# Rotary logits of latent attention: from three products over 64 partitions to two over 128

## The chip, the core and the metric

The kernel runs on one core of a Trainium2 chip. The metric is the device time of one execution in microseconds (us), the median of several runs. The engines are named as in the profile: PE (TensorE's products), PEld (its weight loads), DVE (VectorE), ACT (ScalarE), POOL (GpSimd), SP (SyncE, which issues most DMAs). ACT issues some DMAs, too; such an issue is shown as ACTq.

## What is computed

The program is a model of two blocks. First block: a short convolution mixer, a feed-forward network, latent attention (MLA) over shared keys and values, a second feed-forward network. Second block: a mixer with three branches (spatial gating, stick-breaking attention, dilated attention) and a third feed-forward network. 512 tokens, width 1024, float32. The change is in the latent attention, whose logits have two parts, one of 128 dimensions with keys of each head's own and a rotary one of 64 dimensions with one key for all eight heads:

```python
q = (rms_norm(x_n @ w_dq, q_norm) @ w_uq).reshape(bsz, seq, N_HEADS, QK_NOPE_DIM + QK_ROPE_DIM)
q_nope = q[..., :QK_NOPE_DIM]
q_rope = apply_rope(q[..., QK_NOPE_DIM:], cos[:, None, :], sin[:, None, :])
...
    s = (jnp.einsum('bqhd,bkhd->bhqk', qn, k_nope)
         + jnp.einsum('bqhr,bkr->bhqk', qr, k_rope)).astype(jnp.float32) * scale
    s = jnp.where(k_pos[None, :] <= q_pos[:, None], s, -jnp.inf)
    p = jax.nn.softmax(s, axis=-1).astype(v.dtype)
    return jnp.einsum('bhqk,bkhd->bqhd', p, v)
```

## The kernel before

Every product keeps float32's accuracy by a split: a tile x is cast on ACT to the rounded type fp32r (the high part, xh), DVE subtracts that from x (the low part, xl), and three products are summed in PSUM: high by high, low by high, high by low (`mm3`, lines 155 to 159; `split_to`, lines 119 to 133; the stationary operand is named second in the profile, as in `sc<-kh,qh`). Weights come by DMA from SP as slabs of up to 1 MB into one of two buffers (`raw`, line 139) and are split in the same way (lines 147 and 149, `whi` and `wlo`).

`layer_b` (line 532) holds the attention. It first makes the latent vectors `cq` and `ckv` and the rotary key, `kr` (lines 558 to 560). The key's 64 rows stand twice on the 128 partitions, since its weight columns were doubled. Then it goes over four pairs of heads. `project(pr)` (line 568) makes a pair's operands: a product group for the rotary part of both heads (64 rows each, together 128 partitions, copied to `x` at line 577), two groups for q, two for k, four for v. `rope` (line 522) swaps halves of 32 rows by four small DMAs of 64 KB, issued from ACT (`swap`, lines 518 and 519), and does three operations on DVE (lines 527 to 529); line 596 splits the result into `qr`, tiles `rh` and `rl`. `attend` (line 618) is called once per head: for each of four blocks of 128 queries it makes the logits of 128, 256, 384 or 512 keys in one PSUM tile (`sc`) by six products, three with 128 rows (line 627) and three with the head's 64 rows (line 628), then takes the maximum (line 631, DVE), the exponential (line 633, ACT) and the scaling (line 635, DVE), transposes the block on PE (line 639, `pt`), splits the transposed weights (`pth`, `ptl`) and multiplies them by v (`o`).

While pair pr is attended, the operands of the next pair and the output projection of the pair before (`w_o`, line 606) are there to fill PE. Nothing sets this order by hand: code under `before(start)` gets the priority of an earlier place, and a scheduler at compile time puts the instructions of each engine into a fixed order. Each engine then works through its own in order and waits on semaphores. PSUM has two tiles for `ps` (projections), two for `sc`, three for `pt` and one for `o`.

After the attention comes the second feed-forward network. Its modulation work, which loads the vector c (`cact`, lines 462 to 464) and applies Silu on ACT, may start while the last pair is still attended. The stick-breaking attention of the second block (`stick`, line 964) has products over 64 rows as well.

Of the kernel before, what the change touches and what calls it, by code (L numbers as in the profile page):

```python
# [11 lines left out]
F32 = mybir.dt.float32  # L12
F32R = mybir.dt.float32r
I32 = mybir.dt.int32
AF = mybir.ActivationFunctionType
ALU = mybir.AluOpType
PSUM = bass.MemoryType.PSUM

P = 128
# [3 lines left out]
T = 512  # L23
# [24 lines left out]
class Builder:  # L48
# [483 lines left out]
    def layer_b(self):  # L532
        nc = self.nc
        with ExitStack() as ctx:
            self.psum = self.stat = self.pool("psum_b", 2, ctx, space=PSUM)
            self.pad(480, ctx, side="right")
            self.lat = self.pool("lat", 12, ctx, side="right")
            keep = self.pool("keep_b", 2, ctx, side="right")
            cons = self.pool("const_b", 1, ctx, side="right")
            cos, sin = self.load("cos1", cons), self.load("sin1", cons)  # L540
            mask = self.load("mask_b", cons)
            kr = []
            with ExitStack() as c1:
                self.xs = self.pool("xs_b", 16, c1)
                xq_pool = self.pool("xq", 16, c1)
                self.ph = self.pool("ph_b1", 1, c1)
                xq = self.norm_split("b_mix", xq_pool)
                r4, ms = self.rms_factor(self.h, D)
                rb = self.bcast(r4)
                small = self.s4("small")  # L550
                nc.vector.tensor_scalar(small, ms, EPS, None, ALU.mult)
                xk = self.norm_split("kv_in")

                def rope_k(ps):
                    kr.append(self.t("kr", 1))
                    nc.vector.tensor_tensor(kr[0], ps, rb, ALU.mult)

                cq = self.latent("w_dq", small, "q_norm", 512, xq, pool=self.pool("w_dq", 2, c1))
                ckv = self.latent("w_dkv", small, "kv_norm", 256, xk, rope_k)
                kr = self.split(self.rope(kr[0], cos, sin, self.done), keep, "kr")  # L560
            krh, krl = kr
            with ExitStack() as c2:
                v_pool = self.pool("v", 8, c2)
                k_pool, q_pool, r_pool = self.pool("k", 8, c2), self.pool("q", 8, c2), self.pool("r", 4, c2)
                self.ph = self.pool("ph_b2", 2, c2)
                o_pool = self.pool("o", 8, c2)

                def project(pr):
                    ks, vs, qs = [], [], []
                    for i, (wh, wl) in enumerate(self.slab(self.dr["w_uq"][pr], 512)):  # L570
                        ps = self.ps()
                        for k in range(4):
                            o = k * P
                            self.mm3(ps, wh[:, o:o + P], wl[:, o:o + P], *cq[k], k == 0, k == 3)
                        if i == 0:
                            x = self.t("sq", 2, self.tmp)
                            nc.scalar.copy(x, ps)
                        else:
                            qs.append(self.split(ps, q_pool, "q"))
                    (wh, wl), = self.slab(self.dr["w_ukv"][pr], 1024)  # L580
                    for i in range(2):
                        ps = self.ps()
                        for k in range(2):
                            o = (2 * i + k) * P
                            self.mm3(ps, wh[:, o:o + P], wl[:, o:o + P], *ckv[k], k == 0, k == 1)
                        ks.append(self.split(ps, k_pool, "k"))
                    for b in range(4):
                        ps = self.ps()[:, :256]
                        for k in range(2):
                            o = 512 + 256 * k  # L590
                            ch, cl = (t[:, b * P:(b + 1) * P] for t in ckv[k])
                            self.mm3(ps, ch, cl, wh[:, o:o + 256], wl[:, o:o + 256], k == 0, k == 1)
                        v = v_pool.tile([P, T], F32R, tag="v", name="v")
                        self.split_to(ps, v[:, :256], v[:, 256:])
                        vs.append(v)
                    qr = self.split(self.rope(x, cos, sin, self.done), r_pool, "r")
                    return ks, vs, qs, qr

                ready, outs = project(0), None
                for pr in range(5):  # L600
                    start = self.tc.tile_snap_priority()
                    mine = ready
                    if pr < 3:
                        ready = project(pr + 1)
                    if outs:
                        self.gemm(self.dr["w_o"], outs, self.add_h, (pr - 1,), 4)
                    if pr == 4:
                        break
                    ks, vs, qs, qr = mine
                    outs = []  # L610
                    with self.before(start):
                        for i in range(2):
                            r = slice(64 * i, 64 * i + 64)
                            outs.append(self.attend(qs[i], (qr[0][r], qr[1][r]), ks[i], (krh[r], krl[r]),
                                                    [(v[:, i * P:(i + 1) * P], v[:, 256 + i * P:256 + (i + 1) * P])
                                                     for v in vs], mask, o_pool))

    def attend(self, q, qr, k, kr, vs, mask, o_pool):
        nc = self.nc
        scale = 192 ** -0.5  # L620
        regions = [(0, 0), (1, 0), (2, 0), (2, 256)]
        pts = [self.ps("pt", 3) for _ in range(3)]
        for b in range(4):
            n = (b + 1) * P
            qb = slice(b * P, b * P + P)
            ps = self.ps("sc")[:, :n]
            self.mm3(ps, q[0][:, qb], q[1][:, qb], k[0][:, :n], k[1][:, :n], True, False)
            self.mm3(ps, qr[0][:, qb], qr[1][:, qb], kr[0][:, :n], kr[1][:, :n], False, True)
            s = self.t(f"s{b}", 2, n=n)
            mx, sm = self.s4("mx", 1), self.s4("sm", 1)  # L630
            nc.vector.tensor_tensor_reduce(s, ps, mask[:, T - n:], 1.0, -1e30, ALU.add, ALU.max, mx)
            nc.vector.tensor_scalar(mx, mx, -scale, None, ALU.mult)
            nc.scalar.activation(s, s, AF.Exp, scale=scale, bias=mx, accum_out=sm)
            nc.vector.reciprocal(sm, sm)
            nc.vector.tensor_scalar(s, s, sm, None, ALU.mult)
            for j in range(b + 1):
                t, o = regions[j]
                o += (b - j) * P
                nc.tensor.transpose(pts[t][:, o:o + P], s[:, j * P:(j + 1) * P], self.ident)  # L639
        ph = [self.ph.tile([P, T], F32R, tag="pth", name="pth", bufs=5) for _ in range(3)]  # L640
        pl = [self.ph.tile([P, T], F32R, tag="ptl", name="ptl", bufs=5) for _ in range(3)]
        for i, n in enumerate((512, 384, 384)):
            self.split_to(pts[i][:, :n], ph[i][:, :n], pl[i][:, :n])
        out = self.ps("o", 1)
        for j in range(4):
            t, o = regions[j]
            n = T - j * P
            self.mm3(out[:, j * P:], *vs[j], ph[t][:, o:o + n], pl[t][:, o:o + n], j == 0, j == 3)
        return self.split(out, o_pool, "o")
# [659 lines left out]
```

## Time and profile before

| | us |
|---|---|
| median of 3 runs | 1779.58 |
| lowest and highest run | 1778.07, 1780.67 |
| the profiled execution, its time | 1781.47 |
| its span, first to last instruction | 1779.5 |
| of it PE busy | 1749.2 |
| of it DVE busy | 1110.6 |
| of it ACT busy | 698.3 |
| the first rotary product of the queries starts at | 619.68 |
| the last one starts at | 742.53 |

The views of the profile that are used: the page's table of engines and its costliest groups of instructions; a table of busy time in chosen stretches of the span; the waits of one engine; the timeline, which gives each instruction's start and duration; and the table of DMA issues with the time from issue to landing. A busy time of PE counts modelled ends, and products overlap, so that a product's duration is longer than its distance from the next one's start.

### The profile page before, as it was taken

What the parts mean: (1) busy time and instruction counts of PE and PEld (TensorE: products, weight loads), DVE (VectorE), ACT (ScalarE), POOL (GpSimd) and SP (SyncE); (2) the same over time, 40 slices, a digit from 0 to 9 for tenths busy, and PEclk for the clock granted to TensorE, in tenths of its full rate; (3) what the DMA queues carried; (4) which work ended last, traced back from release to release, by engine and by line L of the source; (5) the groups of instructions that cost most, each with busy time, mean ns of one, the idle gap of its engine ahead of it and who ended that gap; (6) DMA issues with size and microseconds to landing.
All of it is one profiled execution on the core that took longest, in us unless ns stands there. A gap on an engine that the chain in (4) does not pass through costs nothing.

```text
span 1779.5 us, 20603 instructions
## 1 busy us (share of the span) xinstructions
PE 1749.2 (98%) x8261; PEld 1443.9 (81%) x8261; DVE 1110.6 (62%) x1718; ACT 698.3 (39%) x1055; POOL 19.3 (1%) x27
## 2 busy tenths in 40 slices
PE   8999999999999999999999999999999999999998
PEld 7888888888887777787888888877867988888888
DVE  5655699447754676789953775764544766535554
ACT  4323335224433454443432443433354444314432
POOL 0000000000000000000000000100000000000000
PEclk9999999999999999999999999999989999999999
DMA  6222463322231211237423224312101222222231
GB/s 227 95 95 97 164 248 123 114 95 95 97 124 58 89 48 66 94 138 244 144 98 110 96 80 134 114 64 90 63 30 52 80 78 102 84 97 94 105 102 65
DMA packets 38927, 186.57 MB, mean 105 GB/s; under 512 B 5168, under 2 KB 6192, under 8 KB 26672
## 3 DMA queue, kind: packets, MB, share of 16 engines
q1 hardware_dynamic: 36720, 182.38, 29.6%
q10 hardware_dynamic: 2112, 2.89, 0.6%
q8 instruction: 64, 1.05, 0.2%
q14 instruction: 31, 0.25, 0.0%
HBM read 180.27 MB, written 2.10 MB: 102 GB/s over the span
## 4 chain that ended last, share of the span: by engine, by line
PE 90%; DVE 5%; DMA 3%; ACT 1%; issue 1%; POOLq 0%; DVEq 0%; SPq 0%; ACTq 0%
PE ps L157 27%; PE ps L158 27%; PE ps L159 27%; DMA ada<-w_ada 3%; DVE ada L469 2%; DVE wlo L149 1%; PE z L996 1%; PE z L164 1%; PE sc L157 1%; PE o L1004 1%; DVE cv L282 1%; PE sc L159 1%; PE sc L158 1%; PE pt L639 1%; PE sc L860 1%
## 5 line engine op out<-in xcount | busy, mean ns | idle before, releaser
L157 PE MATMUL ps<-xsh,whi 128*128 128x512 f32 (+1 forms) x1448 | 553.8, 387 | 9.7 <-ACT whi L147 6.0
L158 PE MATMUL ps<-xsh,wlo 128*128 128x512 f32 (+1 forms) x1448 | 560.4, 387 | 2.6 <-DVE wlo L149 2.6
L159 PE MATMUL ps<-xsl,whi 128*128 128x512 f32 (+1 forms) x1448 | 557.6, 386 | 0.0
L147 ACT CAST whi<-raw 128x1024 fp32r<-128x1024 f32 (+5 forms) x282 | 297.3, 1059 | 479.1 <-PE ps L159 390.6
L149 DVE TENSOR_TENSOR wlo<-raw,whi 128x1024 fp32r<-128x1024 f32 (+5 forms) x282 | 346.8, 1232 | 92.0 <-ACT whi L147 90.9
L157 PEld LDWEIGHTS ps<-xsh,whi 128*128 128x128 f32 x1448 | 273.4, 189 | 65.0 <-ACT whi L147 6.0
L158 PEld LDWEIGHTS ps<-xsh,wlo 128*128 128x128 f32 x1448 | 273.7, 189 | 60.0 <-DVE wlo L149 5.0
L159 PEld LDWEIGHTS ps<-xsl,whi 128*128 128x128 f32 x1448 | 272.9, 189 | 53.9 <-issue 0.3
L158 PE MATMUL ps<-hidh,wlo 128*128 128x512 f32 (+1 forms) x658 | 241.7, 368 | 0.0
L159 PE MATMUL ps<-hidl,whi 128*128 128x512 f32 (+1 forms) x658 | 241.6, 368 | 0.0
L157 PE MATMUL ps<-hidh,whi 128*128 128x512 f32 (+1 forms) x658 | 241.5, 368 | 0.0
L282 DVE SCALAR_TENSOR_TENSOR cv<-e,par,cv 128x511 f32<-128x511 f32 (+1 forms) x192 | 141.3, 745 | 2.0 <-ACT cv L278 0.3
L157 PEld LDWEIGHTS ps<-hidh,whi 128*128 128x128 f32 x658 | 124.0, 189 | 20.8
L158 PEld LDWEIGHTS ps<-hidh,wlo 128*128 128x128 f32 x658 | 124.0, 189 | 20.7
L159 PEld LDWEIGHTS ps<-hidl,whi 128*128 128x128 f32 x658 | 124.0, 189 | 20.3
L287 DVE TENSOR_TENSOR h<-ps,h 128x512 f32<-128x512 f32 (+1 forms) x75 | 49.9, 668 | 127.8 <-PE ps L159 127.5
L282 DVE SCALAR_TENSOR_TENSOR cv<-ps,par,cv 128x511 f32<-128x511 f32 (+1 forms) x88 | 65.5, 749 | 80.5 <-ACT cv L280 78.9
L414 DVE TENSOR_TENSOR e<-ps,rb 128x512 f32<-128x512 f32 x88 | 60.0, 687 | 57.2 <-PE ps L159 57.2
L126 ACT CAST hidh<-cv 128x512 fp32r<-128x512 f32 x66 | 40.8, 618 | 129.9 <-DVE cv L422 129.9
L278 ACT ACTIVATE cv<-e,par 128x512 f32<-128x512 f32 x96 | 69.0, 721 | 29.9 <-DVE e L414 28.5
L420 ACT ACTIVATE si<-cv 128x512 f32<-128x512 f32 x66 | 41.6, 631 | 75.1 <-DVE cv L282 75.1
L291 DVE SCALAR_TENSOR_TENSOR h<-ps,mod,h 128x512 f32<-128x512 f32 (+1 forms) x38 | 24.0, 636 | 67.5 <-PE ps L159 67.5
(311 smaller groups left out, 1752.7 us busy)
## 6 DMA issues: line engine op xcount, KB each, us to landing
raw<-w_up SPq DMA_DIRECT2D x65, 1024.0 KB, 4.7
raw<-w_down SPq DMA_DIRECT2D x48, 704.0 KB, 4.0
ada<-w_ada SPq DMA_DIRECT2D x48, 512.0 KB, 4.3
raw<-a_w_in SPq DMA_DIRECT2D x9, 1024.0 KB, 4.7
raw<-a_w_out SPq DMA_DIRECT2D x4, 1024.0 KB, 4.6
raw<-w_o SPq DMA_DIRECT2D x4, 1024.0 KB, 5.2
raw<-a_w_in_first SPq DMA_DIRECT2D x8, 384.0 KB, 3.8
raw<-w_uq SPq DMA_DIRECT2D x4, 768.0 KB, 4.8
```

The source lines that it names most:

```text
L126: nc.scalar.copy(vh, src)
L147: nc.scalar.copy(hi[:, :m], raw[:, s])
L149: nc.vector.tensor_tensor(lo[:, :m], raw[:, s], hi[:, :m].bitcast(F32), ALU.subtract)
L157: mm(ps, wh, xh, start=first, stop=False)
L158: mm(ps, wl, xh, start=False, stop=False)
L159: mm(ps, wh, xl, start=False, stop=last)
L278: nc.scalar.activation(y, x, AF.Identity, scale=self.p(w, 2 * n + i))
L282: nc.vector.scalar_tensor_tensor(y[:, k:], x[:, :T - k], self.p(w, (2 - k) * n + i), y[:, k:], ALU.mult, ALU.add)
L287: self.nc.vector.tensor_tensor(self.h[m][:, s], ps, self.h[m][:, s], ALU.add)
L414: nc.vector.tensor_tensor(e, ps, rb, ALU.mult)
L420: nc.scalar.activation(st["s"], y, AF.Silu)
L469: nc.vector.scalar_tensor_tensor(w, w, 1.0, ca, ALU.mult, ALU.mult, accum_out=self.mod[:, i:i + 1])
```

## The change

The query's rotary part is no longer split into two tiles of 128 partitions that hold both heads. A new function, `stacked`, makes one tile `r` of 1024 columns for the pair, 512 for each head. In a head's columns its own 64 partitions hold the high part, and the other 64 hold its low part. The cast writes the high part in place (a cast of 64 partitions per head). DVE subtracts into a tile of its own, `rb`, on the same partitions, and a DMA of 64 partitions by 2 KB, issued from ACT, brings the low part to the other 64 partitions. Since the key stands on both halves, a product of this tile with the high key over all 128 rows gives high by high plus low by high, and a second with the low key gives the remaining term and low by low, which was not computed before. Per block there are two products over 128 rows in place of three over 64. The pool of `r` has two tiles of 1024 columns in place of four of 512.

```diff
-                k_pool, q_pool, r_pool = self.pool("k", 8, c2), self.pool("q", 8, c2), self.pool("r", 4, c2)
+                k_pool, q_pool, r_pool = self.pool("k", 8, c2), self.pool("q", 8, c2), self.pool("r", 2, c2)
...
-                    qr = self.split(self.rope(x, cos, sin, self.done), r_pool, "r")
+                    qr = self.stacked(self.rope(x, cos, sin, self.done), r_pool)
...
-                            r = slice(64 * i, 64 * i + 64)
-                            outs.append(self.attend(qs[i], (qr[0][r], qr[1][r]), ks[i], (krh[r], krl[r]),
+                            outs.append(self.attend(qs[i], qr[:, i * T:i * T + T], ks[i], (krh, krl),
...
+    def stacked(self, x, pool):
+        nc = self.nc
+        t, lo = pool.tile([P, 2 * T], F32R, tag="r", name="r"), self.t("rb", 2, self.tmp, F32R)
+        for i in range(2):
+            own, other = slice(64 * i, 64 * i + 64), slice(64 - 64 * i, 128 - 64 * i)
+            hi = t[:, i * T:i * T + T]
+            nc.scalar.copy(hi[own], x[own])
+            nc.vector.tensor_tensor(lo[own], x[own], hi[own].bitcast(F32), ALU.subtract)
+            nc.scalar.dma_start(hi[other].bitcast(F32), lo[own].bitcast(F32))
+        return t
...
-            self.mm3(ps, qr[0][:, qb], qr[1][:, qb], kr[0][:, :n], kr[1][:, :n], False, True)
+            for part in range(2):
+                nc.tensor.matmul(ps, qr[:, qb], kr[part][:, :n], start=False, stop=part == 1)
```

The compiler's order on PE at the first rotary products of the first pair of heads, before (`ps` is a projection for the next pair, `sc` the logits, `kr` the rotary key):

```order
L159 MATMUL ps<-latl,whi 128x512
L157 MATMUL sc<-krh,rh 128x128
L157 MATMUL sc<-krh,rh 128x256
L158 MATMUL sc<-krh,rl 128x128
L159 MATMUL sc<-krl,rh 128x128
L158 MATMUL sc<-krh,rl 128x256
L159 MATMUL sc<-krl,rh 128x256
L157 MATMUL ps<-lath,whi 128x512
```

And now:

```order
L159 MATMUL ps<-latl,whi 128x512
L641 MATMUL sc<-krh,r 128x128
L641 MATMUL sc<-krl,r 128x128
L641 MATMUL sc<-krh,r 128x256
L641 MATMUL sc<-krl,r 128x256
L157 MATMUL ps<-lath,whi 128x512
```

The place among the projections is the same; four products stand where six were.

The order on ACT at the first pair's rotary operand, before (`sq` is the rotary part, `rh` its high part; the DMAs `rb<-sq` are the swap of the next pair):

```order
L577 COPY sq<-ps 128x512
L147 CAST whi<-raw 128x512
L518 DMA rb<-sq 32x512
L126 CAST rh<-sq 128x512
L519 DMA rb<-sq 32x512
L518 DMA rb<-sq 32x512
L126 CAST qh<-ps 128x512
```

And now:

```order
L577 COPY sq<-ps 128x512
L147 CAST whi<-raw 128x512
L625 CAST r<-sq 64x512 x2
L518 DMA rb<-sq 32x512
L519 DMA rb<-sq 32x512
L627 DMA r<-rb 64x512 x2
L126 CAST qh<-ps 128x512
```

Two casts stand in place of one, and the two DMAs of the low part are behind two of the swap's and ahead of the cast of the next pair's q.

The order on ACT in the last pair, around c's activation (the rows `s` are exponentials of softmax blocks of the last head, `pth` the transposed weights), before:

```order
L126 CAST pth<-pt 128x512
L126 CAST pth<-pt 128x384 x2
L633 ACTIVATE s_5869,sm<-s_5869,mx 128x256
L633 ACTIVATE s_5886,sm<-s_5886,mx 128x384
L147 CAST whi<-raw 128x1024
L633 ACTIVATE s_5904,sm<-s_5904,mx 128x512
L464 ACT_TABLE_LOAD
L464 ACTIVATE cact<-cact 128x1024
```

And now:

```order
L126 CAST pth<-pt 128x512
L126 CAST pth<-pt 128x384 x2
L464 ACT_TABLE_LOAD
L464 ACTIVATE cact<-cact 128x1024
L646 ACT_TABLE_LOAD
L646 ACTIVATE s_5871,sm<-s_5871,mx 128x384
L646 ACTIVATE s_5888,sm<-s_5888,mx 128x512
```

The activation of c moved ahead of the last two exponentials, with a table load on either side of it.

## Rows read from the trace of the kernel before

**Rows 1.** The page: PE; one group of weight loads (count | busy us, mean ns).

```profile
PE 1749.2 (98%) x8261; PEld 1443.9 (81%) x8261; DVE 1110.6 (62%) x1718; ACT 698.3 (39%) x1055; POOL 19.3 (1%) x27
...
L157 PEld LDWEIGHTS ps<-xsh,whi 128*128 128x128 f32 x1448 | 273.4, 189 | 65.0 <-ACT whi L147 6.0
```

**Rows 2.** Busy time by stretches: the attention, and its second pair's part.

```profile
core 0: us, PE busy (x) PEld busy (x) DVE busy (x) ACT busy (x) POOL busy (x), PEclk, DMA share, GB/s
619.60:745.00 125.40, 125.23 (x643) 98.19 (x643) 93.37 (x256) 58.43 (x134) 0.00 (x0) 1.00 0.22 76
645.00:677.00 32.00, 31.84 (x174) 25.66 (x174) 25.57 (x69) 17.27 (x40) 0.00 (x0) 1.00 0.22 76
```

**Rows 3.** Waits of PE from 610 to 755 us: total us, times, longest.

```profile
PE ps L157 <- DVE v L131: 0.2, 1, 0.2
```

**Rows 4.** Timeline of PE around one block: start us, us, engine, line.

```profile
622.42 0.34 PE L159 MATMUL sc<-kl,qh 128*128 128x384 f32 x1
622.69 0.44 PE L157 MATMUL sc<-krh,rh 64*128 64x384 f32 x1
...
623.15 0.33 PE L159 MATMUL sc<-krl,rh 64*128 64x384 f32 x1
623.41 0.50 PE L157 MATMUL ps<-lath,whi 128*128 128x512 f32 x1
623.74 0.39 PE L158 MATMUL ps<-lath,wlo 128*128 128x512 f32 x1
...
624.66 0.39 PE L159 MATMUL ps<-latl,whi 128*128 128x512 f32 x1
624.90 0.40 PE L157 MATMUL sc<-kh,qh 128*128 128x512 f32 x1
```

**Rows 5.** Timeline of PE: full-row products of 256 and 128 columns.

```profile
652.98 0.28 PE L159 MATMUL o<-ptl,v 128*128 128x256 f32 x1
653.10 0.22 PE L157 MATMUL o<-pth,v 128*128 128x128 f32 x1
653.16 0.28 PE L158 MATMUL o<-pth,v 128*128 128x128 f32 x1
653.27 0.27 PE L159 MATMUL o<-ptl,v 128*128 128x128 f32 x1
```

**Rows 6.** Timeline of PE: ends of the first and last run of 64-row products.

```profile
619.36 0.39 PE L159 MATMUL ps<-latl,whi 128*128 128x512 f32 x1
...
620.90 0.40 PE L158 MATMUL ps<-lath,wlo 128*128 128x512 f32 x1
...
741.64 0.39 PE L159 MATMUL sc<-kl,qh 128*128 128x512 f32 x1
...
743.18 0.34 PE L157 MATMUL o<-pth,v 128*128 128x384 f32 x1
```

**Rows 7.** Timeline of ACT, its DMA issues and DVE at the first pair's operand.

```profile
615.52 0.62 ACT L126 CAST rh<-sq 128x512 fp32r<-128x512 f32 x1
617.14 0.51 ACTq L519 DMA_DIRECT2D rb<-sq  x1
...
616.18 0.69 DVE L131 TENSOR_TENSOR rl<-sq,rh 128x512 fp32r<-128x512 f32 x1
```

**Rows 8.** DMA issues at 614.97, 616.21, 617.14 and 734.23: KB, us to landing.

```profile
rb<-sq ACTq DMA_DIRECT2D x1, 64.0 KB, 1.9
...
raw<-w_uq SPq DMA_DIRECT2D x1, 768.0 KB, 5.1
...
rb<-sq ACTq DMA_DIRECT2D x1, 64.0 KB, 4.6
...
cact<-c SPq DMA_DIRECT2D x1, 512.0 KB, 6.2
```

**Rows 9.** Timeline of ACT: a table load, and the last head's output cast.

```profile
745.72 1.28 ACT L464 ACT_TABLE_LOAD   x1
...
753.76 0.59 ACT L126 CAST oh<-o 128x512 fp32r<-128x512 f32 x1 [1.48 <-PE o L159]
```

## The prediction

> **What bounds the kernel now.** I read the page first: PE is busy 98% of the span [rows 1]. [...] Then PE's waits: from 610 to 755 us there is one, of 0.2 us [rows 3]. So an edit here is worth what it takes off PE's own stream, until DVE, ACT or a DMA becomes late. Busy time can't be summed for that, since matmuls overlap and their ends are modelled; I go by the distances between starts.
>
> **The change: PE.** Per head the rotary logits are four blocks of 128, 256, 384 and 512 columns, each now with three products over 64 rows. The timeline of one block [rows 4] shows two costs. First the products: 0.23 us a product for 512 columns, 0.17 for 384 (0.46 for two and the rest of a step below), 0.12 for 256 and 0.11 for 128 [rows 4, 5]. That is 0.63 us a head for one product of each block, 5.0 us over eight heads. Second the change between 64 and 128 rows. The last full-row product of the block starts at 622.42 and the first 64-row one 0.27 later, not 0.17; the next two steps take 0.46, not 0.34; the step back takes 0.26, not 0.17, and the full-row product after it 0.33, not 0.23. Together that is 0.40 us beyond the products. A full-row product that follows a full-row product for another PSUM tile pays nothing: 624.66 to 624.90 is an ordinary step. So I take the row height as the cause.
>
> From the last full-row product before a run of 64-row products to the second after it, less the ordinary steps of these two, the middle example costs 1.32 - 0.17 - 0.23 = 0.92 us, the first run 1.54 - 0.45 = 1.09, the last 1.54 - 0.45 = 1.09 [rows 4, 6]. There are 33 such runs between these two; summed in the same way they cost 27.9 us, of which 15.0 are ordinary steps (three products of 5.0) and 12.8 are changes of height (0.39 a run). After the change there are two products over 128 rows, 10.0 us, and no change of height: **17.8 us less**, 5.0 for products and 12.8 for changes of height. Nothing else on PE covers either, as PE never waits.
>
> **The low part's way to the other 64 partitions.** Per pair of heads one cast and one subtract over 128 partitions become two each over 64, and two DMAs of 128 KB are issued from ACT. An instruction over 64 partitions with the same 512 columns isn't in the trace beside one over 128; bounds are half and all of 0.62 us (ACT) and 0.69 us (DVE) [rows 7]; I take all, since columns are unchanged. That is 2.5 us more of ACT and 2.8 of DVE over four pairs, both beside PE. What reaches the path is the wait for the DMA ahead of a pair's first rotary product, four times.
>
> First pair, where PE's order up to that product is unchanged and it wants the operand at 619.59 (0.23 after 619.36, [rows 6]). The casts come at 615.5 and 616.0 (the one cast is at 615.52 now), the subtracts at 616.18 and 616.8. On ACT two issues for the next pair's swap, about 0.5 and 0.6 us, stand between the casts and the new issue, so it goes out at about 617.2. Beside it in time now is the swap's issue at 617.14, which landed after 4.6 us; an issue at 614.97 landed after 1.9 [rows 7, 8]. The difference is the weight slab of 768 KB that SP issues at 616.21 and that lands after 5.1 [rows 8], at 621.3: the swaps issued after it land just behind it. So the operand is there at 619.1 at best (no stall), by the like row at 621.8, by the slab's whole 5.1 at 622.3: 0 to 2.7 us, and I take 2.2. [...] What queues behind the waiting issues on ACT is the cast of the next pair's q, about a microsecond late; its PSUM buffer is wanted only after the stalled products, so it costs nothing.
>
> Later pairs, counted in the new order with the steps above: from the casts to the first rotary product PE has some 6.7, 5.2 and 5.2 us of other products (in the last pair 36 of W_o stand before it, 24 were there before). The chain takes 1.1 for casts, 0.7 for a subtract, 1.1 for issues ahead (second pair only), and 1.9 to 5.1 for landing: 4.8 to 8.0 in the second pair, 3.3 to 6.9 in the others. In the second and the last pair a W_o slab is issued about 2 us earlier, so the landing is near the middle. I take 0.3, 0 and 0.2; the ends are 0 and 1.3, 1.7, 1.7.
>
> **What else moves.** The compiler's order shifts in three places. (a) In the last pair the Silu table and c's activation now stand before the last two exponentials, so ACT does a table load of 1.28 us [rows 9] twice and c's 1.06 between. PE has 24 products of W_o and one head's values there, about 7.3 us; the transposes that wait for these exponentials come after them: nothing, up to 3 us if c's own load, 6.2 us from issue to landing [rows 8], is late. (b) Three products of W_o that stood behind the last values now stand ahead of them, so less covers the cast that starts at 753.76 [rows 9]: 0 to 1.4 us, I take 0.7. (c) In the stick-breaking stage the order changes a little and has 27 runs of 64-row products, not 26: 0.4 us, ends -1 and +1. Weight loads on SP keep their order.
>
> **Sum:** -17.8 + 2.2 + 0.5 + 0.7 + 0.4 = -14.0 us. On the profiled execution's 1781.47 that is 1767.5; the median of the runs is 1779.58, 1.9 lower, and the change is taken from that: **1765.6 us**.
>
> **The rivals.**
> *DVE becomes the bound.* It has 93.4 us of work there and gets 2.4 more (four subtracts of about 0.6 back to back), in a stretch that shrinks to some 110 us. That is 87%; in the second pair's 32.00 us it is 25.57 now and 26.2 in 27.6 later, 95%. For it: a softmax block passes DVE four times, with two PSUM buffers for logits. Against: PE hides all of it now at 80% in that same stretch, and logits come earlier, too. If DVE can't be filled beyond those 80%, the stretch takes 95.8 / 0.80 = 119.8, a gain of 5.6 less the 1.1 of (b) and (c): about 1775.
> *The changes of height don't go away*, because something else in that place costs the time or because it hid waits that now appear. Then only the 5.0 remain, less 3.8: 1778.4, no change that can be measured. Against it: the ordinary step at 624.66 [rows 4]. [...]
> *Slower: the low part's DMAs are late in all four pairs.* The mechanism is the one of the first pair: a small DMA behind a weight slab, with PE's in-order stream in front of it. It decides from a mean stall of (17.8 - 1.1) / 4 = 4.2 us a pair (5.1 for slower by 0.2%). If PE stood at the product as the casts begin, the chain would take up to 8.0 us, four times, 32 us: 1779.6 - 16.7 + 32 = 1795. Against it: only the first pair has so short a lead.
>
> **How the numbers follow.** Forecast 0.72, with its own range 1761 to 1770 (no stall at all; ends of the unknown costs). DVE 0.15, height stays 0.08, DMAs late 0.05. Faster by over 0.2% (3.6 us, about what a measurement of this kernel can tell from no change) is 0.72 + 0.15 = 0.87, within 0.08, slower 0.05. The range that holds it 8 times in 10 takes in most of DVE's case: 1761 to 1773.5.
>
> **What would show it.** Right: rotary products with 128 rows, starts at 0.11 to 0.23 us with ordinary steps on both sides, the attention's stretch some 13 us shorter, one PE wait of about 2 us for a DMA at the first pair. Wrong: steps beside the rotary products that stay at 0.26 to 0.33; PE waits on DVE across the stretch; a wait of 3 us or more for the low part in every pair; PE waiting for the last exponentials behind the table loads.

## The result and the profile after

| | before | after |
|---|---|---|
| median of 7 runs each, us | 1780.67 | 1772.91 |
| lowest and highest run, us | 1778.07, 1788.16 | 1769.03, 1776.60 |
| profiled execution and its span, us | 1781.47, 1779.5 | 1773.94, 1772.2 |

The ratio of after to before is 0.9947, 95% interval 0.9934 to 0.9961: 9.4 us less (6.9 to 11.8). The forecast was 14.0 less. The direction and the cause hold; about a third of the expected gain is missing.

The table of engines of the changed kernel (busy us, share of the span, instructions), and the group of weight loads that [rows 1] shows:

```profile
PE 1735.4 (98%) x8229; PEld 1441.1 (81%) x8229; DVE 1112.5 (63%) x1722; ACT 702.8 (40%) x1061; POOL 19.9 (1%) x27
...
L157 PEld LDWEIGHTS ps<-xsh,whi 128*128 128x128 f32 x1448 | 273.1, 189 | 66.0 <-ACT whi L147 6.1
```

32 products fewer, as foreseen, and DVE and ACT 2 and 4.5 us busier. Then PE's waits from 610 to 755 us, the stretch of [rows 3] (us in total, times, longest):

```profile
PE sc L641 <- DMA r<-rb: 2.8, 2, 2.6
PE ps L157 <- DVE v L131: 1.2, 1, 1.2
PE ps L157 <- ACT oh L126: 0.7, 1, 0.7
PE ps L157 <- DVE h L287: 0.6, 1, 0.6
PE o L159 <- DVE ptl L131: 0.4, 1, 0.4
```

Before there was one wait of 0.2. The first row is the forecast's stall: 2.6 us ahead of the first pair's rotary products, and 0.2 ahead of the second pair's. What PE does there is in its timeline (start us, us, engine, line, operation, in brackets the idle time ahead and what ended it), the place that answers to [rows 4, 6]:

```profile
624.38 0.30 PE L641 MATMUL sc<-krh,r 128*128 128x128 f32 x1 [2.59 <-DMA r<-rb]
624.51 0.27 PE L641 MATMUL sc<-krl,r 128*128 128x128 f32 x1
624.63 0.33 PE L641 MATMUL sc<-krh,r 128*128 128x256 f32 x1
624.79 0.28 PE L641 MATMUL sc<-krl,r 128*128 128x256 f32 x1
624.91 0.39 PE L157 MATMUL ps<-lath,whi 128*128 128x512 f32 x1
...
625.85 0.63 PE L158 MATMUL ps<-lath,wlo 128*128 128x512 f32 x1
626.27 0.63 PE L159 MATMUL ps<-latl,whi 128*128 128x512 f32 x1
...
629.43 0.39 PE L157 MATMUL ps<-lath,whi 128*128 128x512 f32 x1
629.65 0.39 PE L158 MATMUL ps<-lath,wlo 128*128 128x512 f32 x1
```

The rotary products now have 128 rows and ordinary steps: 0.12 and 0.16 us, and 0.12 to the projection behind them. But from 625.85 on a product of 512 columns takes 0.43 us to the next, and from 629.43 again 0.22. The table of stretches says why (us, busy time and count of PE, PEld, DVE, ACT, POOL, then the granted clock, share and rate of the DMAs):

```profile
624.30:627.00 2.70, 2.62 (x11) 2.28 (x12) 1.97 (x8) 0.53 (x2) 0.00 (x0) 0.78 0.47 173
627.00:629.00 2.00, 2.00 (x7) 1.90 (x7) 0.69 (x1) 1.97 (x3) 0.00 (x0) 0.50 0.00 0
629.00:631.00 2.00, 2.00 (x9) 1.61 (x9) 1.33 (x8) 1.51 (x6) 0.00 (x0) 0.94 0.00 0
```

Behind the 2.6 us in which PE did nothing the granted clock is at 0.50 for about 3.4 us (an estimate from these rows): a share of 0.22 of the 2.70 us is lost, 0.50 of the next 2.00 and 0.06 of the last 2.00, which is 1.7 us in all. The forecast has no such term.

The operand's way, as the timeline shows it for ACT, its DMA issues and DVE (they answer to [rows 7]):

```profile
617.39 0.62 ACT L625 CAST r<-sq 64x512 fp32r<-64x512 f32 x1
...
618.03 0.62 ACT L625 CAST r<-sq 64x512 fp32r<-64x512 f32 x1
618.84 1.22 ACTq L627 DMA_DIRECT2D r<-rb  x2
...
618.13 1.40 DVE L626 TENSOR_TENSOR rb<-sq,r 64x512 fp32r<-64x512 f32 x2
```

An operation over 64 partitions takes as long here as one over 128 in [rows 7], as taken: 0.62 us on ACT for 0.62, 0.70 on DVE for 0.69. The DMA issues around it (KB, us to landing), which answer to [rows 8], from two tables: issues at 618.24 and 618.84, and the third pair's at 672.25.

```profile
raw<-w_uq SPq DMA_DIRECT2D x1, 768.0 KB, 5.8
r<-rb ACTq DMA_DIRECT2D x2, 128.0 KB, 5.2
...
r<-rb ACTq DMA_DIRECT2D x2, 128.0 KB, 2.3
```

By the trace's landing times the slab is there at 624.07, the first low part, issued 0.6 us behind it, at 624.24; with no slab ahead the same DMA takes 2.3 us. What the queues moved in between is in the DMA table (queue 1 is SP's, queue 10 is ACT's; packets, MB, share of the 16 engines): first from 619.5 to 621.0, where queue 10 has no packet at all, then from 621.0 to 624.3.

```profile
q1 hardware_dynamic: 77, 0.47, 88.9%
...
q10 hardware_dynamic: 256, 0.39, 40.6%
```

So for 1.5 us the DMA engines brought 0.47 MB by the slab's queue and nothing of the small DMAs beside it; queue 10's 0.39 MB came in the 3.3 us from 621.0 on. The casts come 1.9 us later than the forecast had them (617.39, not 615.5), and PE is ready 2.0 us later, too (621.6, not 619.59).

### The profile page after: what moved, and what is told of

Its sections match the earlier page's. It is cut to its first block, busy times and chain, and to the rows that moved or that the text cites. A ratio compares the mean times of both kernels' runs of the same rounds, so it can differ in the third digit from the quotient of the medians.

```text
span 1772.2 us, 20573 instructions
## 1 busy us (share of the span) xinstructions
PE 1735.4 (98%) x8229; PEld 1441.1 (81%) x8229; DVE 1112.5 (63%) x1722; ACT 702.8 (40%) x1061; POOL 19.9 (1%) x27
## 4 chain that ended last, share of the span: by engine, by line
PE 87%; DVE 7%; DMA 4%; ACT 1%; issue 1%; ACTq 0%; DVEq 0%; POOLq 0%; SPq 0%
PE ps L157 26%; PE ps L158 26%; PE ps L159 26%; DMA ada<-w_ada 3%; DVE ada L469 2%; DVE wlo L149 1%; DVE cv L282 1%; PE z L164 1%; PE z L1009 1%; PE o L1017 1%; PE sc L641 1%; DMA r<-rb 1%; ACT whi L147 1%; PE sc L873 1%; PE pt L652 0%
```

## Where the time is: one stretch, eleven kernels

Eleven kernels, two of them profiled more than once, are compared over the same stretch of PE, "the attention" below: from the first product of the latent vectors with the queries' weights (`ps<-lath`) to the last product of W_o (`ps<-ol`), by their starts. These are the stretches of before, of after and of three kernels of the next section (two full-row products; low part first; no low-part DMA):

```profile
591.75:765.46 173.71, 169.93 (x858) 133.77 (x857) 130.07 (x314) 83.47 (x176) 1.39 (x1) 1.00 0.23 76
```

```profile
592.33:757.60 165.27, 156.37 (x825) 132.28 (x825) 130.59 (x318) 86.44 (x181) 1.38 (x1) 0.98 0.27 87
```

```profile
592.59:750.18 157.59, 152.78 (x826) 130.36 (x825) 127.71 (x314) 82.72 (x176) 1.39 (x1) 1.00 0.25 84
```

```profile
591.90:750.54 158.64, 152.90 (x826) 130.02 (x825) 130.22 (x318) 86.62 (x181) 1.38 (x1) 1.00 0.28 90
```

```profile
591.99:748.23 156.24, 152.30 (x826) 130.38 (x825) 129.72 (x318) 84.93 (x180) 1.38 (x1) 1.00 0.25 85
```

From such rows, with the sum of PE's waits in the stretch (3.7 us before) and the time lost at the lower clock in it, comes the table below. "Rest" is the difference to before, less the added waits, less the clock's loss: what the products and the changes of row height are worth. Then comes the "stick stretch", some 500 us later: from the first product behind PE's wait of 3.6 us in the stick-breaking block to the end of that block's products. Last is the ratio of the runs to before. Each stretch is from one profile, the ratio from all the runs.

| kernel | attention | to before | added waits | clock | rest | stick stretch | ratio (95%) |
|---|---|---|---|---|---|---|---|
| before | 173.7 | | | | | 88.1 | 1 |
| after | 165.3 | -8.4 | +5.0 | +3.4 | -16.8 | 87.9 | 0.9947 (0.9934 to 0.9961) |
| after, second time | 164.3 | -9.4 | +5.6 | +1.7 | -16.7 | 90.2 | 0.9952 (0.9938 to 0.9965) |
| after, third time | 163.7 | -10.0 | +4.9 | +1.7 | -16.6 | 90.3 | 0.9953 (0.9935 to 0.9971) |
| three full-row products | 162.6 | -11.1 | -0.3 | +1.7 | -12.5 | 88.0 | 0.9923 (0.9907 to 0.9939) |
| two of three products | 168.7 | -5.0 | +1.3 | 0 | -6.3 | 93.6 | 0.9995 (0.9982 to 1.0008) |
| two full-row products | 157.6 | -16.1 | +0.9 | 0 | -17.0 | 89.6 | 0.9922 (0.9904 to 0.9941) |
| no low-part DMA | 156.2 | -17.5 | +0.3 | 0 | -17.8 | 88.9 | 0.9905 (0.9887 to 0.9924) |
| stacked early | 162.8 | -10.9 | +5.6 | 0 | -16.5 | 92.5 | 0.9961 (0.9944 to 0.9977) |
| small slab | 160.9 | -12.8 | +3.5 | 0 | -16.3 | 92.5 | 0.9961 (0.9947 to 0.9975) |
| low part first | 158.6 | -15.1 | +1.8 | 0 | -16.9 | 86.2 | 0.9940 (0.9926 to 0.9954) |
| the same again | 158.6 | -15.1 | +2.1 | 0 | -17.2 | 90.1 | 0.9933 (0.9917 to 0.9948) |
| zero key | 162.4 | -11.4 | +1.2 | 0 | -12.6 | 88.4 | 0.9945 (0.9930 to 0.9959) |
| seven outputs | 174.8 | +1.1 | +1.2 | 0 | -0.1 | 93.5 | 1.0033 (1.0022 to 1.0045) |

Of the 3.4 us in the first row of after, 1.7 are from 605 to 609 (0.55 from 605.0 to 608.6), behind a wait for `lath` that before has, too (2.4 and 2.1 us; before is at 1.00 from 603.0 to 619.6); the other two profiles of after have the same wait (2.4, 2.1), and their 1.7 us are the ones behind the low part's wait. Only these 1.7 are in all three.

## The experiments

**The two terms of the gain.** Before without one of the three products, still over 64 rows:

```diff
-            self.mm3(ps, qr[0][:, qb], qr[1][:, qb], kr[0][:, :n], kr[1][:, :n], False, True)
+            nc.tensor.matmul(ps, qr[0][:, qb], kr[0][:, :n], start=False, stop=False)
+            nc.tensor.matmul(ps, qr[1][:, qb], kr[0][:, :n], start=False, stop=True)
```

> The kernel before, with the last of the three 64-row products (high query by low key) left out; it leaves out that part of the rotary logits. The heights still change. Theory (products cost 5.0 us a set, changes of height 12.8): 5 us below the kernel before, less what a new order costs, 0.2 to 0.3%. Rival (the gain of the changed kernel comes from its fewer products, changes of height cost nothing that ends last): the whole gain, 8 to 9 us.

Measured: 1782.42 us, ratio 0.9995: as a time, a miss. In the attention the product is worth its price (-5.0, or -6.3 beside 1.3 of new waits); in the profile the 93.6 us of the stick stretch, where before has 88.1, take it back. That is taken up below.

Before with all three products over 128 rows, PE's order as before:

```diff
-                            r = slice(64 * i, 64 * i + 64)
+                            r = slice(0, 128)
```

> The kernel before, with each of its three rotary products over all 128 partitions, so that a head's logits hold the rotary part of both heads of the pair; nothing else changes, no DMA is added, and the order on PE is the same. Theory: no change of height, 12.8 us less PE time, and with the same order few new waits: 9 to 13 us below the kernel before. Rival (height costs nothing): no difference, within 1 us.

Measured: 1770.57 us, ratio 0.9923, 13.7 us less than before's 1783.23 by the ratio (a little more than the 9 to 13 expected), with as many products of as many columns. The waits of PE from 591 to 754 us in it:

```profile
PE ps L157 <- ACT lath L126: 2.0, 1, 2.0
PE ps L157 <- DVE h L287: 1.0, 2, 0.6
PE sc L157 <- ACT kh L126: 0.2, 1, 0.2
PE ps L157 <- DVE v L131: 0.2, 1, 0.2
```

They are before's. So changing between 64 and 128 rows costs, as [rows 4, 6] had it: 12.5 us in the attention, 12.8 forecast. Both edits at once:

```diff
-                            r = slice(64 * i, 64 * i + 64)
+                            r = slice(0, 128)
...
-            self.mm3(ps, qr[0][:, qb], qr[1][:, qb], kr[0][:, :n], kr[1][:, :n], False, True)
+            nc.tensor.matmul(ps, qr[0][:, qb], kr[0][:, :n], start=False, stop=False)
+            nc.tensor.matmul(ps, qr[1][:, qb], kr[0][:, :n], start=False, stop=True)
```

> Before with two rotary products over all 128 rows on before's own tiles, no casts by halves and no DMA for a low part (the logits then hold both heads' rotary parts, and lack the product with the key's low part). It has the unfavourable order of the stick-breaking stage, too. Theory: the attention is 17.8 us shorter, less up to 2 us of new waits, so 16 to 18 at full clock; the stick-breaking stretch gives 4.5 to 5.5 back; in all 11 to 13 less, ratio 0.9933. Rival (products and changes of height hid other work): the attention is 12 us or less shorter, waits on DVE and ACT fill the rest.

Measured: 1770.41 us, ratio 0.9922. The attention is 16.1 us shorter with 0.9 of new waits: 17.0 for both terms, 17.8 forecast. The stick stretch gives back 1.5 us in its profile, not the 4.5 to 5.5 expected.

**The low part's DMA.** After without these DMAs; the 64 partitions that they fill are zero, so the low part is left out:

```diff
-            nc.scalar.dma_start(hi[other].bitcast(F32), lo[own].bitcast(F32))
```

> The changed kernel without the two DMAs per pair: the other 64 partitions stay zero, so the low part of the query is left out of the rotary logits. Casts, subtracts and products are all there. Theory (what the change gives back is mostly the wait for the low part): about 4 to 6 us below the changed kernel, 1767 to 1769, 12 to 14 below the kernel before. Rival (DVE or the order gives it back): within 1.5 us of the changed kernel.

Measured: 1767.28 us, ratio 0.9905 (17 us less than before, where 12 to 14 were expected), the attention 17.5 us shorter, with all casts and subtracts in place. So the DMAs, not the 2.5 us more of ACT and 2.8 of DVE, are what after pays for. PE's order in the attention is another here than in after, and in the next three kernels, too, so a small part of their added waits can be the order's. Next, the weight slab ahead of the first pair's DMAs cut to a third:

```diff
-        nc.sync.dma_start(raw[:, :n], src)
+        nc.sync.dma_start(raw[:, :512 if third else n], src[:, :512] if third else src)
...
-            s = slice(o, o + m)
+            s = slice(0, 512) if third else slice(o, o + m)
...
-                    for i, (wh, wl) in enumerate(self.slab(self.dr["w_uq"][pr], 512)):
+                    for i, (wh, wl) in enumerate(self.slab(self.dr["w_uq"][pr], 512, third=pr == 2)):
```

> After, but of the weight slab that is issued 0.6 us ahead of the first pair's low-part DMAs (the third pair's query weights, 768 KB) only the first 256 KB are loaded, and used three times, so the third pair's queries come from the wrong weights; instructions are otherwise as many. Theory (the low part lands with the slab ahead of it, and the granted clock falls behind the wait): the landing takes 2 to 3 us instead of 5.4, PE's wait for it goes from 2.6 to 0.5 us or less, the clock stays at 1.00 from 621 to 631 us, and the run is about 4 us shorter than after: ratio to before 0.9925. Rival (a DMA from one half of the partitions to the other takes that long by itself there): landing 5 us, wait 2.6, ratio 0.9947 as after.

Its DMA issues (KB, us to landing), and the first rotary product in its timeline:

```profile
raw<-w_uq SPq DMA_DIRECT2D x1, 256.0 KB, 3.4
r<-rb ACTq DMA_DIRECT2D x2, 128.0 KB, 2.9
```

```profile
622.83 0.30 PE L641 MATMUL sc<-krh,r 128*128 128x128 f32 x1 [0.28 <-DMA r<-rb]
```

The low part lands earlier with the slab (0.3 us behind it), the first pair's wait goes from 2.6 to 0.28, and the clock does not fall there (1.00 from 622 to 631 us). Another wait grows. The second pair's low part goes out 0.8 us behind a slab of W_o (1.3 in after) and is late by 1.4 us (0.2 in after):

```profile
651.03 0.33 PE L641 MATMUL sc<-krh,r 128*128 128x128 f32 x1 [1.41 <-DMA r<-rb]
```

In the attention 2.8 to 4.4 us are won against after's three profiles (160.9), as the theory has it. The run is not faster (1776.79, ratio 0.9961), which the theory did not expect: its stick stretch is 92.5, and its profile enters the attention 1.8 to 3.8 us later than after's.

Then the order of the issues turned round: the first pair's low part from SP, the slab behind it.

```diff
-        nc.sync.dma_start(raw[:, :n], src)
+        with self.tc.issue_after(behind) if behind else nullcontext():
+            nc.sync.dma_start(raw[:, :n], src)
...
-                    for i, (wh, wl) in enumerate(self.slab(self.dr["w_uq"][pr], 512)):
+                    for i, (wh, wl) in enumerate(self.slab(self.dr["w_uq"][pr], 512, behind=self.first_low if pr == 2 else None)):
...
-                    qr = self.stacked(self.rope(x, cos, sin, self.done), r_pool)
+                    qr = self.stacked(self.rope(x, cos, sin, self.done), r_pool, nc.scalar if pr else nc.sync)
...
-            nc.scalar.dma_start(hi[other].bitcast(F32), lo[own].bitcast(F32))
+            dma = queue.dma_start(hi[other].bitcast(F32), lo[own].bitcast(F32)).ins
+            if queue is nc.sync:
+                self.first_low = dma
```

> After, with the first pair's two low-part DMAs issued from SP, and the 768 KB slab queued behind them on SP instead of 0.6 us ahead of them. Theory (landing with the slab): low part lands about 2.2 us after its issue, PE's wait for it is 0.5 us or less instead of 2.6, the clock stays at 1.00 behind it, the slab comes 1 to 1.5 us later and is waited for by nobody; about 4 us less than after, ratio 0.9925. Rival one: landing 5 us all the same, ratio 0.9947. Rival two: the wait only moves, to the slab's products or to DVE, and the sum of PE's waits between 600 and 760 us stays within 1 us of after's.

Its DMA issues, PE's waits in the attention (lines are one higher in this kernel), and the stretch behind the first rotary product:

```profile
raw<-w_uq SPq DMA_DIRECT2D x1, 768.0 KB, 4.5
r<-rb SPq DMA_DIRECT2D x2, 128.0 KB, 2.4
```

```profile
PE ps L158 <- ACT lath L126: 1.7, 1, 1.7
PE ps L158 <- DVE v L131: 1.3, 1, 1.3
PE ps L158 <- DVE h L288: 1.0, 2, 0.5
PE ps L158 <- ACT oh L126: 0.7, 1, 0.7
PE o L160 <- DVE ptl L131: 0.4, 1, 0.4
PE sc L158 <- ACT kh L126: 0.4, 1, 0.4
```

```profile
619.60:625.00 5.40, 5.40 (x30) 4.64 (x29) 4.55 (x19) 4.61 (x11) 0.00 (x0) 1.00 0.60 228
```

No wait for `r` at all, the granted clock at 1.00, nobody waits for the slab: 15.1 us off the attention. The second pair's low part, too, now goes out ahead of its slab of W_o (at 638.08, the slab at 640.00), and it lands after 2.4 us instead of 5.6. The median is 1772.35 us, ratio 0.9940 (0.9925 expected), beside 1775.27 and 0.9952 for after on the same chip:

> After itself once more, beside the others. Both theories: 0.9947 of before within 0.0015. If the granted clock outside the attention is what differs between runs of one kernel, span times mean granted clock agrees between this and the earlier runs of after within 1 us (1759.1), while the times spread over 5 us or more. Rival: the spread is in waits, and span times clock spreads as much.

As expected of after's repeat, its time is the first one's by the ratio, and span times mean granted clock agrees with the first (1758.3 and 1759.1, each a mean over the runs); its times spread over 4.2 us, a little less than the 5 expected. Once more, with after beside it a third time:

> The version with the first pair's low-part DMAs ahead of the slab once more, with after beside it on the same chip. Theory: 0.994 of before, 2.5 to 4 us less than after. Rival (the difference between the two was one of granted clock alone): the same as after within 1 us.

> After itself a third time, beside the version with the low part first. Both: 0.995 of before; span times mean granted clock 1758 to 1760.

Measured: 1771.77 us (0.9933) against 1774.64 (0.9953). Both pairs say 3 us in favour of the low part first, at the lower end of the 2.5 to 4 that were expected, and less than the 5 to 7 won in the attention. The intervals of the ratios overlap. Span times mean granted clock, an estimate of the time at full clock, tells the two apart, but for a small overlap: 1752.9 to 1757.5 us in the eleven runs of the low part first, 1756.6 to 1762.7 in the eighteen of after, with means of 1755.9 and 1758.8. So the low part first is the better version, by about 3 us. Part of the difference is given back in the feed-forward network behind the attention, where PE waits for the split weights; from 750.6 to 1143.6 us in this kernel's second profile

```profile
PE ps L159 <- DVE wlo L150: 3.3, 7, 1.2
```

and from 757.7 to 1148.7 us in after's:

```profile
PE ps L158 <- DVE wlo L149: 2.2, 3, 1.4
```

The clock's fall is in after's second and third profile as well, behind waits of 2.7 and 2.6 us for the low part; from 624 to 626 us each:

```profile
624.00:626.00 2.00, 2.00 (x6) 1.71 (x6) 0.64 (x4) 0.67 (x2) 0.00 (x0) 0.50 0.00 0
```

```profile
624.00:626.00 2.00, 2.00 (x7) 1.77 (x8) 1.52 (x6) 0.00 (x0) 0.00 (x0) 0.50 0.58 229
```

**More time for the first pair instead.** After, with the first pair's stacked query written ahead of its v:

```diff
+                    if pr == 0:
+                        qr = self.stacked(self.rope(x, cos, sin, self.done), r_pool)
                     for b in range(4):
```

> The changed kernel with the first pair's rotation and stacking written ahead of its four value groups, so that its low parts are on their way before the next weight slab is asked for. Theory (the changed kernel gives back 2.6 us in one wait for the low part behind a slab, and some 2 us more in products at half clock just after it): this wait and the half clock after it go, 4 to 5 us below the changed kernel, 1767 to 1769 us. Rival (DVE bounds the attention, the wait only stands in for it): waits move to other places, same time as the changed kernel within 1.5 us.

Measured: 1777.36 us, ratio 0.9961: no gain. The first pair's wait is gone, and the fall of the clock with it (1.00 over the attention): its low parts are issued at 611.3 and 612.0, ahead of the slab at 617.4, and land after 2.2 us, and the first rotary product, at 615.34, follows the one before it without a wait. In its place PE waits for the split of v twice ahead of that product (1.0 and 1.2 us; with a third one 3.5 us in all, 1.2 in after). And the second pair's low part, issued 0.8 us behind a slab of W_o, is now late by 1.2 us:

```profile
648.60 0.33 PE L644 MATMUL sc<-krh,r 128*128 128x128 f32 x1 [1.19 <-DMA r<-rb]
```

```profile
raw<-w_o SPq DMA_DIRECT2D x1, 1024.0 KB, 6.0
r<-rb ACTq DMA_DIRECT2D x2, 128.0 KB, 5.9
```

Added waits are 5.6 us, much as in after (4.9 to 5.6). So the waits moved, as the rival has it: to DVE, 2.3 us more for v than in after, and for 1.2 us to the same wait for a low part behind a slab, in another pair.

**Three products without any DMA.** Before, with a key for each head of a pair whose other half is zero:

```diff
+            kz = [[keep.tile([P, T], F32R, tag="kr", name=f"kr{x}") for x in "hl"] for _ in range(2)]
+            for i in range(2):
+                for z in kz[i]:
+                    nc.gpsimd.memset(z[64 - 64 * i:128 - 64 * i].bitcast(F32), 0.0)
...
-                o_pool = self.pool("o", 8, c2)
+                o_pool = self.pool("o", 6, c2)
...
-                            outs.append(self.attend(qs[i], (qr[0][r], qr[1][r]), ks[i], (krh[r], krl[r]),
+                            outs.append(self.attend(qs[i], qr, ks[i], kz[i],
```

> Before, with all three rotary products over 128 rows: for each head of a pair a key of its own whose other 64 partitions are zero, written once; no DMA for a low part. Room for the two keys more comes from six buffers instead of eight for the heads' outputs. Theory (the changes of height cost 12.8 us, the third product 5.0, and the stacked query's DMA has given back more than the third product is worth): ratio 0.9925, about 13 us less than before and 4 less than after. Rival (stacking is worth its DMA, two products beat three): slower than after, ratio above 0.9955. If six output buffers are too few, PE waits for ps of W_o or o appear in the second half of the attention.

Measured: 1773.26 us, ratio 0.9945, between the two theories. The attention's 12.6 of rest are the changes of height again. So the whole of what stacking adds to that, a product less, is spent on its DMA in after: the two have the same ratio.

**The stretch 500 us later.** The kernels with two of three products, the small slab and the early stacked query have one order of PE in the stick-breaking block, different from before's and after's, though no line of that block was touched: the scheduler's choices there hang on what came ahead. Two full-row products have it as well. One buffer less for the heads' outputs gives this order to before:

```diff
-                o_pool = self.pool("o", 8, c2)
+                o_pool = self.pool("o", 7, c2)
```

> Before with seven buffers for the heads' outputs instead of eight. The attention's order changes only from the third pair on; but the compiler's order of TensorE in the stick-breaking stage some 500 us later becomes the one that the kernels with an early stacked query, with two of three products and with the small slab have there, and that the others haven't. Theory (that order costs time and was what swallowed the gains of these three): the attention takes 158.7 us within 1.5, the stick-breaking stretch that took 103.1 takes 107.6 to 108.7, the run is 4 to 6 us longer than before, ratio 1.0025 to 1.003. Rival (their losses came from elsewhere): stretch and time as before, ratio 1.000.

Its stick stretch, and before's:

```profile
1299.94:1393.43 93.49, 93.49 (x412) 70.88 (x413) 41.55 (x74) 44.73 (x85) 0.00 (x0) 0.90 0.09 32
```

```profile
1295.06:1383.14 88.08, 88.08 (x412) 67.72 (x413) 41.41 (x74) 44.31 (x85) 0.00 (x0) 0.94 0.12 36
```

The same number of products takes 5.4 us longer, and the run is 6.2 us slower (1789.02 against 1782.85, ratio 1.0033). Time by granted clock is 93.49 x 0.90 = 84.1 and 88.08 x 0.94 = 82.8: about 1 us is the order's own, the rest is the lower clock. In the five kernels with this order the stretch takes 89.6 to 93.6 us, in the others 86.2 to 90.3. In four of the five the stretch has a mean granted clock of 0.90 or 0.91, with two full-row products 0.94. With seven outputs and with two of three products the clock falls once more some 43 us into the stretch, where PE had not waited since its start (0.57 from 1343 to 1347 us, 0.66 from 1335 to 1340); in before it is 1.00 from 1320 to 1360 and in after's first profile from 1312 to 1375. The attention's own 1.1 us here are waits for v (1.4 in all, 0.2 before), within the 1.5 that were allowed for (the expectation counts both stretches from other products).

So the order costs time, but less than this profile says. The profiled run is one of the slowest of its twelve (1792.24 us) and lost 17.9 us to the clock (span times one minus the mean granted clock); the twelve lost 13.7 on average, before's seventeen runs 11.8. That leaves about 2 us of the 6.2 to the clock and 4.2 to the rest, of which the profiles show 1.1 in the attention, 1 in the stick stretch and 1.5 between the two. How much of the gains of the other kernels went this way is therefore not shown to the microsecond; two of three products, too, lost 14.5 us to the clock on average beside before's 12.4. Why the clock falls more in one run of a kernel than in another is open: after alone has stick stretches of 87.9, 90.2 and 90.3 us.

## Why the prediction was right, and where its sum was off

Right in kind: faster, within the wide range, and for the reason given. Wrong in size: 14.0 us forecast, 9.4 measured. That the time is still in the range is partly luck: it is outside the forecast's own 1761 to 1770, and the range went up to 1773.5 for the case in which DVE becomes the bound, which did not come. Step by step:

- **Products and changes of height, -17.8.** The rest column has 16.3 to 17.2 us in the kernels with the DMA, 17.0 and 17.8 in those without: right within 1.5 us. Heights apart 12.5 and 12.6 (12.8 forecast), the product apart 6.3 (5.0). The rival by which the heights don't go away fell with the three full-row products. Nor did a product over 128 rows pay its weight load in full: the rotary products above start 0.12 to 0.16 us apart, with a load of 0.19 us each.
- **First pair's wait, +2.2.** It was 2.6 to 2.7 us in three profiles, by the mechanism named (landing with the slab: 5.2 us behind 768 KB, 2.9 behind 256 KB, 2.4 ahead of it). In the 1.5 us from 619.5 in which 77 packets of the slab's queue went through, ACT's queue had none. **This term was mis-sized by what follows it:** 1.7 us at the lower clock behind the wait. Priced with it the stall is 4.3 to 4.4 us, twice the forecast, and in the attention the low part first wins all of it back.
- **Later pairs, +0.5.** 0.2 to 0.4 in the second pair, whose DMA was 5.6 to 5.8 us under way behind a slab of W_o, nothing in the others (2.2 to 2.3 us). That this wait is short is a matter of when the two are issued: it was 1.2 and 1.4 us in the two kernels with 0.8 us between them.
- **What else moves, +0.7 and +0.4.** (b) came as a wait of 0.7 for `oh`, but before has one of 0.6 for `h` in the same place: from the last values to the last W_o product both take 12.0 us. So 0. (a) cost nothing. (c) -0.2 in the stretch above.
- **Not in the sum:** waits for DVE. v, +1.0 in the last pairs; `ptl`, 0.4; and `h`, 1.0 at the first product behind the attention. They stay in the kernel with the low part first.
- **DVE becomes the bound.** The time of this rival, 1775, worked out from [rows 2], is nearer to the result than the forecast, but not by its mechanism: in the attention DVE is busy for 79% in after (130.59 of 165.27), and with the low part first for 82%, in 6.6 us less. PE's waits for DVE went up by 1.4 us in the attention, not by some 9.
- **Slower, with the DMAs late in all pairs,** fell: of four pairs only the first waits for more than 0.4 us.

In sum, for the attention: -16.7, +4.9 to +5.6 of waits (3.4 forecast), +1.7 of clock, and another 1.7 of clock in one profile of three: -8.4 to -10.0 where -14.4 was forecast. Outside it after's first profile is 1.1 us longer than before's (0.4 forecast), the other two 3.3 and 7.9, with more time at the lower clock.

How far the granted clock enters a median can be estimated from the runs: span times mean granted clock is 1759.1, 1758.3 and 1758.9 us in the three sets of runs of after (7, 5 and 6), while their times go from 1769.0 to 1779.2; before's sets give 1769.1, 1768.6 and 1768.8 (19, 11 and 17). By this estimate the change is worth 10 us at full clock. The like figures are 1766.4 for two of three products (2.7 less than before), 1757.5 for three full-row products, 1754.8 for two, 1754.1 without the low part's DMA, 1760.3 with the small slab, 1761.7 stacked early, 1756.1 and 1755.8 with the low part first, 1759.2 with the zero key, and 1773.0 with seven outputs.

## What to carry to other kernels

On an engine without idle time, compare steps, not durations: a run of products over 64 rows between products over 128 cost 0.38 us here beyond its products, and products over 128 rows took no longer than over 64 (in before's timeline 0.23 to 0.24 us from start to start for 512 columns and 0.12 for 256, with either height), so filling the array (even with zeros) is the first thing to try. A small transfer on the path should be issued ahead of the large one (it landed after 2.4 us here), not 0.6 us behind it (5.2 us). Price a stall of TensorE with the products behind it (1.7 us here, beside 2.6 of waiting), and a changed order with every stage that the scheduler orders after it. And where the granted clock differs from run to run, compare span times mean granted clock over all runs before a single profile is believed.

## What the runs showed of the chip

- A DMA of 128 KB issued 0.6 us behind a slab on another queue landed 0.2 to 0.5 us after the slab, whether that had 768 KB (three profiles) or 256 KB (one). Issued 1.3 us ahead of the slab on the same queue, it landed after 2.4 us.
- PE idle for 2.6 to 2.7 us ahead of the rotary products was followed by a granted clock of 0.50 in three profiles of three (1.7 us lost each). PE idle for 2.4 us ahead of 604 us was followed by 0.55 in after's first profile, and 1.7 us are lost in the attention of three full-row products, where that wait (2.0) is the longest; behind the same wait before (2.1) is at 1.00, and after's second and third profile (2.4 and 2.1) lose no more than the 1.7 above. What tells these apart the runs don't show.
- The 412 or 413 products recorded of the stick-breaking block took 86.2 to 93.6 us, at a mean granted clock of 0.96 to 0.90, with one and the same wait of 3.6 us of PE ahead of them. In two profiles of one order the clock fell once more, to 0.57 and 0.66, with PE at work for some 43 us.
